# A second group of seven products per feed-forward, with the sums of weight blocks made by adding transfers

## The chip, the cores and the metric

The kernel runs on one core of one Trainium2 chip. The metric is the device time of one execution in microseconds (us), as the median of several runs. The core has five engines that work side by side, each with its own queue of instructions: TensorE (in the profile PE; PEld is its weight load), VectorE (DVE), ScalarE (ACT), GpSimd (POOL) and SyncE (SP), which here only issues transfers. Transfers between the main memory (DRAM) and the on-chip memory run on 16 transfer engines (DMA).

## The reference

A trunk of two layers on 256 tokens of width 1024, all in float32. Each layer is a sandwich of feed-forward, mixer, feed-forward; the first layer's mixer is a convolution module, the second's a latent attention. The change touches the feed-forwards, of which there are four:

```python
def swiglu_ffn(h, w1, w3, w2):
    return (jax.nn.silu(h @ w1) * (h @ w3)) @ w2

for i in range(DEPTH):                       # DEPTH = 2
    h = h + 0.5 * swiglu_ffn(rmsnorm(h, ffn_norm1[i]), ffn1_w1[i], ffn1_w3[i], ffn1_w2[i])
    m = rmsnorm(h, mix_norm[i])
    h = h + (conv_module(m, ...) if i == 0 else mla(m, ...))
    h = h + 0.5 * swiglu_ffn(rmsnorm(h, ffn_norm2[i]), ffn2_w1[i], ffn2_w3[i], ffn2_w2[i])
return rmsnorm(h, final_norm)
```

`w1` and `w3` are 1024 x 2816, `w2` is 2816 x 1024.

## The kernel before

**Blocks.** Weights come as blocks of 128 x 2048 float32 (one megabyte), in a fixed list `blocks`, in the order of use. A block is fetched into one of four raw buffers (tag `raw`, `RAW_BUFS = 4`) and then split into a high part `hi` (a rounding copy on ScalarE) and a low part `lo` (raw minus high, on VectorE), each in two pieces of 1024 columns (`PIECES = 2`). Five pairs of `hi` and `lo` exist (`W_BUFS = 5`). Activations are split in the same way (`Xh`, `Xl`; `Gh`, `Gl`). Every product of two float32 tiles is three matmuls (`mm3`): high times low, high times high, low times high.

**The first product** (`h @ w1` and `h @ w3` together) runs over six chunks `c` of output columns: 0 to 4 with 512 columns of each of the two matrices, 5 with 256. A plain chunk of 512 is four blocks (two halves of the rows of the weights for each matrix). Its 2 x 2 x 2 block products of 12 matmuls are 96 matmuls into four accumulator banks: two matrices by two blocks of 128 tokens.

**A group of seven.** In the chunks listed in `SEVEN_UP`, and in the first four blocks of every second product (`SEVEN_DOWN`), the eight block products of this 2 x 2 by 2 x 2 block matrix product are replaced by seven, in the manner of Winograd and Strassen: some factors are sums of weight blocks, some are sums of row blocks ("forms"), and the results are combined between banks. That makes 84 matmuls. `seven(four)` puts seven entries in the list, `load_seven` makes the j-th factor of the weights, `seven_products` runs the products, `sums_of_rows`, `whole_rows` and `forms_of` make the forms of the rows. Before, there is one such chunk in each first product, chunk 3, and one group in each second product: eight groups. `load_seven` fetches the four blocks once each (L185) and makes four in-place differences of whole blocks on VectorE (L201). The forms of chunk 3 are made when chunk 1 begins; their whole rows take a raw buffer for a while.

**The start of feed-forwards two to four.** The two blocks of 128 tokens become ready one after the other. The rows of the second block are turned by a round trip through DRAM (`turn_blocks`, L489 writes, L494 reads); `X.begin()` first calls `raw_to`, which fills free raw buffers with coming blocks (L181), and then issues these turns. `first_chunk` runs chunk 0 in an order of its own; when its third part is done being laid out, it calls `load_ahead()`, which brings in the blocks up to three ahead of those in use. Fetches in `load` (L239) and `fetched` are ordered behind the last turned read:

```python
dma = nc.sync.dma_start(raw, src)
if turns:
    order(dma, turns[-1].ins)
```

**What sets the order.** The program is laid out by a planner that fills each engine's queue from its own estimate of times, with priority to what stands earlier in the code; `urgent` raises the priority, `order(a, b)` puts a behind b in a queue without a wait at run time. `behind` keeps splits behind the latest urgent instructions. `gates` are the splits of a chunk's outputs after their turn (`turn`, L862); `seven_products` orders them among the weight splits.

## Time and profile before

| | us |
|---|---|
| median of 3 runs | 892.14 (891.55 to 892.82) |
| the profiled execution, whole | 891.44 |
| its span in the trace | 889.5 |
| feed-forward two, first product begins | 272.1 |
| feed-forward three, first product begins | 446.2 |
| feed-forward four, first product begins | 708.7 |

The page shows one profiled execution. Busy time of an engine excludes the instructions that only issue transfers or wait. A group of instructions is given with its line, engine, operation, the names of what it writes and reads, its count, its busy time, the mean duration in ns, and the idle time of its engine before it with what ended that. Rows of stretches give: the stretch, its length, busy time and count for PE, PEld, DVE, ACT and POOL, the granted clock of TensorE, the busy share of the transfer engines, and GB/s. Rows of one line of the code give durations in ns (min/median/max) and the first and last start; "DMA to landing" gives min/median/max from issue to landing. Rows in order of time give start, length, engine, line, operation, count.

### The profile page before, as it was taken

The numbers are of one execution on the slowest core, as the hardware profiler recorded it, in microseconds if no ns is written. First come the engines' busy times: TensorE is split into PE (matmuls) and PEld (weight loads), VectorE is DVE, ScalarE is ACT, GpSimd is POOL, SyncE is SP. The second block draws the span as 40 slices with busy tenths as digits, with TensorE's granted clock in tenths as the row PEclk, the third lists the DMA queues.
The fourth block names the chain that finished last, engine by engine and source line by source line (L and its number), as shares of the span: only waits on it lengthen the run. The fifth ranks groups of instructions, "written<-read, shape, count | busy, mean of one in ns | idle before, by whom it ended". The sixth has DMA issues, their size and how long they took to land.

```text
span 889.5 us, 12294 instructions
## 1 busy us (share of the span) xinstructions
PE 882.0 (99%) x4209; PEld 741.9 (83%) x4209; DVE 770.4 (87%) x1114; ACT 580.2 (65%) x1005; POOL 104.8 (12%) x227
## 2 busy tenths in 40 slices
PE   9999999999999999999999999999999999999997
PEld 7888887898988888888888888888899888888886
DVE  6899999789999998999498989995778689989973
ACT  7667868789887655657275465673676666474752
POOL 1000000079952000000010000001400010000000
PEclk9999999999999999999999999999999999999999
DMA  9884929834216855939759378495643549287541
GB/s 338 297 308 161 398 80 374 300 132 153 96 60 225 307 213 194 365 93 393 251 179 344 97 249 318 142 386 183 221 147 142 190 155 368 80 300 276 192 190 48
DMA packets 71054, 198.94 MB, mean 224 GB/s; under 512 B 12368, under 2 KB 41936, under 8 KB 51664
## 3 DMA queue, kind: packets, MB, share of 16 engines
q1 hardware_dynamic: 70560, 197.47, 61.9%
q8 instruction: 33, 0.54, 0.2%
q10 hardware_dynamic: 432, 0.69, 0.2%
q14 instruction: 29, 0.24, 0.1%
HBM read 181.87 MB, written 16.25 MB: 223 GB/s over the span
## 4 chain that ended last, share of the span: by engine, by line
PE 98%; DVE 1%; issue 0%; ACT 0%; ACTq 0%; DVEq 0%
PE u L333 17%; PE u L337 17%; PE u L336 17%; PE o L333 9%; PE o L337 9%; PE o L336 9%; PE u L1019 3%; PE gate L1019 3%; PE o L1255 3%; PE u L418 2%; PE sc L1616 1%; PE tp L453 1%; PE pairs L1062 1%; DVE lo L201 1%; PE a L337 1%; PE a L336 1%
## 5 line engine op out<-in xcount | busy, mean ns | idle before, releaser
L248 DVE TENSOR_TENSOR lo<-raw,hi 128x1024 fp32r<-128x1024 f32 (+1 forms) x228 | 266.8, 1210 | 29.2 <-ACT hi L247 28.5
L247 ACT CAST hi<-raw 128x1024 fp32r<-128x1024 f32 (+1 forms) x230 | 228.5, 1044 | 72.1 <-DMA raw<-in_f2w 24.3
L337 PE MATMUL u<-hi,Xl 128*128 128x512 f32 x592 | 230.4, 389 | 0.0
L336 PE MATMUL u<-hi,Xh 128*128 128x512 f32 x592 | 230.3, 389 | 0.0
L333 PE MATMUL u<-lo,Xh 128*128 128x512 f32 x592 | 230.2, 389 | 0.0
L215 ACT CAST hi<-raw 128x1024 fp32r<-128x1024 f32 x112 | 111.7, 1049 | 56.7 <-DVE raw L201 46.4
L201 DVE TENSOR_TENSOR lo<-raw,hi 128x1024 fp32r<-128x1024 f32 x112 | 132.0, 1215 | 6.6 <-ACT hi L215 6.5
L337 PEld LDWEIGHTS u<-hi,Xl 128*128 128x128 f32 x592 | 111.1, 188 | 23.6 <-DVE Xl L472 0.5
L336 PEld LDWEIGHTS u<-hi,Xh 128*128 128x128 f32 x592 | 111.1, 188 | 23.1
L333 PEld LDWEIGHTS u<-lo,Xh 128*128 128x128 f32 x592 | 111.1, 188 | 22.9
L333 PE MATMUL o<-lo,Gh 128*128 128x512 f32 (+1 forms) x276 | 106.7, 386 | 0.0
L336 PE MATMUL o<-hi,Gh 128*128 128x512 f32 (+1 forms) x276 | 106.5, 386 | 0.0
L337 PE MATMUL o<-hi,Gl 128*128 128x512 f32 (+1 forms) x276 | 106.5, 386 | 0.0
L444 POOL TENSOR_TENSOR ms<-ss 128x1 f32<-128x1 f32 x16 | 8.1, 509 | 592.8 <-ACT junk L436 592.8
L201 DVE TENSOR_TENSOR raw<-raw,raw 128x2048 f32<-128x2048 f32 x32 | 73.1, 2285 | 0.8 <-DMA raw<-in_f1w 0.2
L333 PEld LDWEIGHTS o<-lo,Gh 128*128 128x128 f32 x276 | 51.8, 188 | 10.6 <-DVE lo L201 0.2
L337 PEld LDWEIGHTS o<-hi,Gl 128*128 128x128 f32 x276 | 51.8, 188 | 10.5
L336 PEld LDWEIGHTS o<-hi,Gh 128*128 128x128 f32 x276 | 51.8, 188 | 10.4
L1108 DVE SCALAR_TENSOR_TENSOR acc<-V,dw,acc 128x128 f32<-128x128 f32 (+1 forms) x174 | 53.9, 390 | 0.0
L970 ACT ACTIVATE s<-u,R 128x512 f32<-128x512 f32 (+1 forms) x48 | 30.9, 647 | 29.5 <-PE u L337 28.7
L1129 ACT ACTIVATE prod<-V,dw 128x128 f32<-128x128 f32 (+1 forms) x128 | 45.6, 415 | 1.9 <-POOL Y L1130 1.0
L806 DVE SCALAR_TENSOR_TENSOR h<-o,rh,h 128x512 f32<-128x512 f32 (+1 forms) x18 | 12.9, 719 | 29.0 <-PE o L337 29.0
(269 smaller groups left out, 1306.6 us busy)
## 6 DMA issues: line engine op xcount, KB each, us to landing
raw<-in_f2w SPq DMA_DIRECT2D x66, 1024.0 KB, 5.6
raw<-in_f1w SPq DMA_DIRECT2D x62, 1024.0 KB, 6.9
raw<-in_cw SPq DMA_DIRECT2D x12, 1024.0 KB, 5.2
gd<-gt SPq DMA_DIRECT2D x160, 64.0 KB, 2.9
gb<-gd SPq DMA_DIRECT2D x24, 256.0 KB, 2.8
rows<-gd SPq DMA_DIRECT2D x16, 256.0 KB, 3.3
raw<-in_wo SPq DMA_DIRECT2D x4, 1024.0 KB, 4.7
hd<-rows SPq DMA_DIRECT2D x56, 64.0 KB, 2.3
```

The source lines that it names most:

```text
L201: ins = nc.vector.tensor_sub(out, left, right)
L215: casts[n, i] = nc.scalar.copy(hi[:, c], raw[:, c]), sub(lo[:, c], raw[:, c], hi[:, c].bitcast(F32))
L247: casts[len(loaded), i] = (nc.scalar.copy(hi[:, c], raw[:, c]), low.tensor_sub(lo[:, c], raw[:, c], hi[:, c].bitcast(F32)))
L248: low.tensor_sub(lo[:, c], raw[:, c], hi[:, c].bitcast(F32)))
L333: mm = nc.tensor.matmul(o, ah, bl, start=start, stop=False, skip_group_check=seeded)
L336: nc.tensor.matmul(o, ah, bh, start=False, stop=False, skip_group_check=seeded)
L337: return nc.tensor.matmul(o, al, bh, start=False, stop=stop, skip_group_check=seeded)
L970: nc.scalar.activation(s[:, :w], u[0, tb][:, :w], AF.Silu, scale=X.r[tb])
L1019: mm = nc.tensor.matmul(u[:, t], w[:, c], X.x[:, k, t], start=(k == 0), stop=(k == KT - 1))
L1108: dve_last.append(nc.vector.scalar_tensor_tensor(out if j == j1 - 1 else y, v, w, y, op0=ALU.mult, op1=ALU.add))
L1129: prods_last.append(nc.scalar.activation(p, v, AF.Copy, scale=w))
L1255: p = nc.tensor.matmul(o[tb, d], (Zl if kind == "x" else Zh)[:, f, tbs(tb)], (lo if kind == "l" else hi)[:, c], start=(f, kind) == (0, "l" ...
```

## The change

`SEVEN_UP` gets chunk 1 beside chunk 3 for feed-forwards two to four: eleven groups instead of eight. The differences of weight blocks become sums, and the sums are made by transfers issued from GpSimd that add into a raw buffer. The signs of the forms and of the combinations between banks are changed to match. Of the four blocks f0 to f3, the group now fetches d = f2, y = f1, c = f0 and x = f0; it adds f3 into y and f1 into x. The seven factors are x, c, d, x, y, c, x: before the fourth, f3 is added into x; before the sixth, c is fetched anew with f3; before the seventh, f2 is added into x. That is five plain and four adding transfers per group, where four plain ones were.

The order of the products changes too: the first is now one with a form of the rows (and x), and product 2 is cut in two halves of six matmuls with product 3 between them. The forms are made at chunk 0 where chunk 1 is a group. `raw_to` now stops at a block that is a tuple (a group's entry). The buffers of the turned blocks with tag `g` become three, the orderings of the gates are fitted, and in the attention the scores of heads one and two are ordered behind those of the head before.

```diff
-SEVEN_UP = {0: (3,), 1: (3,), 2: (3,), 3: (3,)}
+SEVEN_UP = {0: (3,), 1: (1, 3), 2: (1, 3), 3: (1, 3)}
...
     def raw_to(last):
         while len(loaded) + len(raws) < last:
             src = blocks[len(loaded) + len(raws)]
-            assert not isinstance(src, tuple)
+            if isinstance(src, tuple):
+                break
...
-    def fetched(src):
-        raw = rawp.tile([P, HB], F32, tag="raw", name=uid("raw"))
+    def fetched(src, raw=None):
+        if raw is None:
+            raw = rawp.tile([P, HB], F32, tag="raw", name=uid("raw"))
         dma = nc.sync.dma_start(raw, src)
         if turns:
             order(dma, turns[-1].ins)
...
         if j == 0:
-            b[11], b[12] = fetched(four[0]), fetched(four[1])
-        elif j == 1:
-            b[22] = fetched(four[3])
-        elif j == 2:
-            b[21] = fetched(four[2])
...
-        if j == 1:
-            sub(b[11], b[12], b[11])
-            sub(b[12], b[22], b[12])
-        elif j == 2:
-            thirds[n] = sub(b[11], b[22], b[11])
+            b["d"], b["y"], b["c"], b["x"] = (fetched(four[i]) for i in (2, 1, 0, 0))
+            nc.gpsimd.dma_start(b["y"], four[3], accum_op=ALU.add)
+            nc.gpsimd.dma_start(b["x"], four[1], accum_op=ALU.add)
+        elif j == 3:
+            nc.gpsimd.dma_start(b["x"], four[3], accum_op=ALU.add)
+        elif j == 5:
+            fetched(four[3], b["c"])
         elif j == 6:
-            sub(b[11], b[21], b[11])
-        raw = b[(11, 11, 11, 21, 12, 22, 11)[j]]
+            nc.gpsimd.dma_start(b["x"], four[2], accum_op=ALU.add)
+        raw = b["xcdxycx"[j]]
...
-        sums = [(0, x22, x21, x22, ALU.add), (2, x21, x11, x21, ALU.subtract), (1, x11, x22, x11, ALU.subtract),
-                (3, x12, x12, x11, ALU.subtract)]
+        sums = [(0, x22, x21, x22, ALU.subtract), (2, x21, x11, x21, ALU.subtract),
+                (1, x11, x22, x11, ALU.subtract), (3, x12, x12, x11, ALU.add)]
...
-        product(rows(0, 0), c11, True)
-        first = urgent(nc.scalar.copy)(c21, c11)
+        product(0, forms[0], c22, True)
+        kept = tmp.tile([P, 512], F32, tag="s", name=uid("p5"))
+        first = urgent(nc.scalar.copy)(kept, c22)
...
+        product(1, rows(0, 0), c11, True)
+        urgent(nc.scalar.copy)(c21, c11)
+        product(2, rows(1, 0), c11, False, range(2))
+        product(3, forms[1], c21, False)
+        product(2, rows(1, 0), c11, False, range(2, 4))
+        add = urgent(nc.vector.tensor_sub)(c12, kept, c21)
...
+        product(4, forms[2], c21, False)
+        add = urgent(nc.vector.tensor_sub)(c22, kept, c21)
+        product(5, forms[3], c12, False)
...
+        product(6, rows(1, 1), c21, False)
...
-            if seven_up and c == min(seven_up) - 2:
+            if seven_up and c == max(min(seven_up) - 2, 0):
...
-            last = None
+            last = score_last[-1] if 0 < hd < 3 else None
```

More of the change, by code (lines that the diff above doesn't have):

```diff
@@ L387, in seven_products @@
         n0 = n_used[0]
-        before = []
+        before, parts = [], {}
         c11, c21, c12, c22 = banks[0, 0], banks[1, 0], banks[0, 1], banks[1, 1]
-        product(rows(0, 0), c11, True)
-        first = urgent(nc.scalar.copy)(c21, c11)
+        product(0, forms[0], c22, True)
+        kept = tmp.tile([P, 512], F32, tag="s", name=uid("p5"))
+        first = urgent(nc.scalar.copy)(kept, c22)
         for cast in late.values():
             order(cast, first.ins)
-        product(forms[0], c22, True)
-        kept = tmp.tile([P, 512], F32, tag="s", name=uid("p5"))
-        urgent(nc.scalar.copy)(kept, c22)
-        product(forms[1], c21, False)
-        add = urgent(nc.vector.tensor_add)(c12, c21, kept)
-        order(casts[n0 + 5, 0][1], add.ins)
-        for high, low in gates[-2 * NT:-NT] if not late else ():
-            order(low, thirds[n0 + 2].ins)
+        product(1, rows(0, 0), c11, True)
[4 more added lines that the diff above has]
+        add = urgent(nc.vector.tensor_sub)(c12, kept, c21)
+        order(casts[n0 + 6, 0][1], add.ins)
+        for high, low in gates[max(len(gates) - 2 * NT, gates_from[0]):-NT] if not late else ():
+            order(low, casts[n0 + 2, PIECES - 1][1].ins)
         late_gates = []
@@ L411, in seven_products @@
             order(low, casts[n0 + 7, PIECES - 1][1].ins)
-        product(forms[3], c12, False)
-        product(rows(1, 1), c21, False)
+        order(casts[n0 + 7, 0][1], add.ins)
+        product(6, rows(1, 1), c21, False)
     def some(o, kinds, ah, al, bh, bl, start, stop):
```

28 lines of the change are left out of this document (13 added, 15 removed).

## The prediction

> **What bounds the kernel now.** I read the page from the top: the shares, the transfer queues, the chain that ended last, the groups of instructions, the transfer issues.
>
> ```profile
> span 889.5 us, 12294 instructions
> ...
> PE 882.0 (99%) x4209; PEld 741.9 (83%) x4209; DVE 770.4 (87%) x1114; ACT 580.2 (65%) x1005; POOL 104.8 (12%) x227
> ...
> DMA packets 71054, 198.94 MB, mean 224 GB/s; under 512 B 12368, under 2 KB 41936, under 8 KB 51664
> ...
> q1 hardware_dynamic: 70560, 197.47, 61.9%
> ...
> PE 98%; DVE 1%; issue 0%; ACT 0%; ACTq 0%; DVEq 0%
> ...
> L248 DVE TENSOR_TENSOR lo<-raw,hi 128x1024 fp32r<-128x1024 f32 (+1 forms) x228 | 266.8, 1210 | 29.2 <-ACT hi L247 28.5
> L247 ACT CAST hi<-raw 128x1024 fp32r<-128x1024 f32 (+1 forms) x230 | 228.5, 1044 | 72.1 <-DMA raw<-in_f2w 24.3
> ...
> L444 POOL TENSOR_TENSOR ms<-ss 128x1 f32<-128x1 f32 x16 | 8.1, 509 | 592.8 <-ACT junk L436 592.8
> L201 DVE TENSOR_TENSOR raw<-raw,raw 128x2048 f32<-128x2048 f32 x32 | 73.1, 2285 | 0.8 <-DMA raw<-in_f1w 0.2
> ...
> raw<-in_f1w SPq DMA_DIRECT2D x62, 1024.0 KB, 6.9
> ```
>
> The chain is TensorE (PE) for 98% of the span. VectorE (DVE) is busy 87%, and yet nothing waits for it: less VectorE work by itself saves nothing. Only fewer matmuls, or a stall of TensorE, can move the time. What one matmul is worth is its share of a whole first product, not its modelled duration, since matmuls overlap. These are the stretches of busy time of the first products of feed-forwards two, three and four:
>
> ```profile
> 272.10:389.10 117.00, 117.00 (x518) 96.85 (x517) 108.58 (x118) 68.58 (x91) 3.21 (x4) 1.00 0.70 250
> 446.20:563.20 117.00, 117.00 (x518) 96.87 (x517) 107.92 (x118) 69.28 (x92) 3.21 (x4) 1.00 0.65 231
> 708.70:825.70 117.00, 116.98 (x518) 96.55 (x516) 107.39 (x121) 70.85 (x97) 3.35 (x8) 1.00 0.64 227
> ```
>
> The code issues 516 matmuls there (four chunks of 96, one of 84, one of 48; the row counts two more that overlap its edges), without a hole and at a granted clock of 1.00: 117.0/516 = 0.2267 us each. A product of a group of seven (12 matmuls) takes 2.72 us, a plain chunk of 96 takes 21.8 us. So chunk 1, which becomes a group of seven, starts today at 293.9, 468.0 and 730.5.
>
> **The change, part by part.** *Matmuls.* Three chunks go from 96 to 84: 36 x 0.2267 = 8.2 us saved, all on the path. Nothing else in the change can save more than a fraction of a microsecond, since TensorE has no idle time to give back.
>
> *VectorE and ScalarE.* The 32 subtractions on raw blocks go: 32 x 2.285 = 73.1 us of VectorE, off the path, worth 0. Three chunks have seven blocks to split into high and low halves instead of four: 9 blocks, two pieces each, 18 x 1.21 = 21.8 us of VectorE and 18 x 1.04 = 18.8 us of ScalarE, covered by the 51 us that VectorE is relieved of on balance and by ScalarE's idle 35%. Worth 0.
>
> *Where the first transfers of chunk 1 can start.* This is the step that I think decides. Today chunk 1 is plain, and its first raw blocks are fetched ahead by the function that fills the raw buffers before the second token block is turned. In the changed code that function stops at a block of a group. The group's fetches are issued later, and by the ordering in the fetch helper they stand on SP's queue behind the read of the last turned block. That read goes out here (the SP queue in order of time):
>
> ```profile
> 278.83 0.34 SPq L494 DMA_DIRECT2D rows<-hd  x1
> 279.21 13.03 SPq L239 DMA_DIRECT2D raw<-in_f2w  x5
> ```
> ```profile
> 451.69 0.34 SPq L494 DMA_DIRECT2D rows<-hd  x1
> 452.07 14.44 SPq L239 DMA_DIRECT2D raw<-in_f1w  x4
> ```
> ```profile
> 717.96 0.34 SPq L494 DMA_DIRECT2D rows<-hd  x1
> 718.41 0.37 SPq L717 DMA_DIRECT2D gf<-in_gfin  x1
> ```
>
> So t0, the issue of the group's first fetch, is 279.2, 452.1 and 718.4: 14.7, 15.9 and 12.1 us ahead of chunk 1. In that time four fetches (d, y, c, x, in this order, with x last), one adding transfer into x, and the split of x must be done, because the first product uses x. Three fetches issued together at 279.2 landed like this:
>
> ```profile
> L239 SPq DMA_DIRECT2D raw<-in_f2w x3: 364/432/433, 279.2 to 280.2; - x3
> ...
> DMA to landing us min/median/max: 4.9/7.0/8.9
> ```
>
> The first landed at 279.2+4.9 = 284.1, the third at 280.2+8.9 = 289.1: 2.5 us apart. The fourth, x, then lands at t0+12.4.
>
> *The price of an adding transfer.* No transfer of this kind is in the trace; call it A from issue to landing. The lower bound is the best plain megabyte, the upper bound the worst fetch of a group:
>
> ```profile
> L181 SPq DMA_DIRECT2D raw<-in_f2w x5: 327/328/328, 247.4 to 704.8; - x5
> ...
> DMA to landing us min/median/max: 4.7/4.9/7.2
> ```
> ```profile
> L185 SPq DMA_DIRECT2D raw<-in_f2w x16: 327/333/432, 303.5 to 809.0; - x16
> ...
> DMA to landing us min/median/max: 5.3/7.6/9.5
> ```
>
> I take 6.9, the median of the 62 megabyte fetches of this weight tensor (last row of the first fence): same size, same source and destination, with other traffic beside them, as the add into x has the one into y beside it. Bounds 4.7 and 9.5. The Trainium skill (DMA: Bandwidth & Descriptors, "Anatomy of one DMA — SWDGE (gpsimd) path") gives 2.0 us plus the bytes over 436 GB/s for a transfer issued from GpSimd, an estimate of 4.4 us for a megabyte; by it the sum below would be 902. The plain megabytes of this trace never beat 4.7.
>
> *The first product.* The first half of x is split after 1.04 (high) + 1.21 (low) = 2.3 us. Product 0 starts at t0+12.4+6.9+2.3 = t0+21.6: 300.8, 473.7, 740.0, late by 6.9, 5.7 and 9.5 us, together 22.1.
>
> *The later sums in x.* The next add may go out only when the split of x is finished, 1.2 us after its first half; then 6.9 and 2.3 again: 10.4 us from product 0 to product 3. TensorE has 2.5 products between them (0, 1 and half of 2), 6.8 us: a stall of 3.6. From product 3 to product 6 it has 3.5 products, 9.5 us: a stall of 0.9. Together 4.5, times three, 13.5.
>
> *The other eight groups* (chunk 3 and the second product, everywhere) get the same chain, with more time ahead. In chunk 3 of feed-forward three the fetches go out here:
>
> ```profile
> L185 SPq DMA_DIRECT2D raw<-in_f1w x4: 327/340/352, 479.0 to 488.0; - x4
> ...
> DMA to landing us min/median/max: 6.1/7.9/8.1
> ```
>
> The last of the four lands at 488.0+8.1 = 496.1 at worst; +6.9+2.3 = 505.3, against 511.6 for product 0 (446.2 + 3 x 21.8). Product 3 is ready at 515.7 (needed 518.4), product 6 at 526.1 (needed 527.9): hidden, with 1.8 us to spare at the end. I price them at 0; three adds share that margin, so it is gone when A passes 7.5, and at 9.5 each of these groups would stall about 6 us.
>
> *Forms of the rows.* They are now needed by product 0 of chunk 1, and their sum takes a raw buffer, free when d is split:
>
> ```profile
> L352 DVE TENSOR_TENSOR xs<-Xh,Xl 128x2048 f32<-128x2048 f32 x4 | 9.1, 2286 | 0.0
> L345 DVE TENSOR_TENSOR xs<-xs 128x512 f32<-128x512 f32 x16 | 10.9, 683 | 0.0
> ```
>
> d at t0+4.9, split +3.5, sum +2.3, first form +0.7 and its own split about +1.3: t0+12.7, covered by x's chain (t0+21.6). If that cover went, it would still be in time in two of the three.
>
> *Order of the products, copies between banks.* A half product (1.36 us) stands behind each copy or subtraction:
>
> ```profile
> L259 DVE TENSOR_TENSOR u<-u,p x2: 693/696/700, 520.8 to 525.3; 128x512 f32<-128x512 f32 x2
> ...
> L259 ACT COPY u<-u x1: 570/570/570, 514.5 to 514.5; 128x512 f32<-128x512 f32 x1
> ```
>
> 0.57 and 0.70 fit in 1.36: 0. *Queues.* The adds wait on POOL's queue; behind them stand only the norms' small operations (L444), whose next turn comes after the second product's plain blocks. The repeated fetch of c waits on SP for the split of c; behind it stand chunk outputs, not read before the second product. Both 0. The order of two heads' scores and the third buffer for turned blocks move no work: 0.
>
> *Sum.* 22.1 + 13.5 - 8.2 = +27.4 us. The profiled execution took 891.4 us (span 889.5), 0.7 under the median 892.1; so 918.8 against its own time, **919.5** against the median. With A = 4.7: late by 4.7, 3.5, 7.3, and 1.4 at each product 3, +11.5, 904. With A = 9.5: 29.9 + 3 x (6.2+3.5) - 8.2 = +50.8, 943.
>
> **The rivals.** *Faster: the loads go out earlier than I think.* The raw buffers of the group are free long before t0 (today they hold prefetched blocks), and only the order on SP holds the fetches back. Were they issued as the buffers come free, x would land about 10 us sooner, every stall of the first groups would be covered, and the gain of 8.2 would remain: 884. It breaks even when x lands 27.4/3 = 9.1 us earlier in each. Against it: the three pairs of rows above show weight fetches or others right behind that read, as the ordering demands. The groups of chunk 3 show that with more time ahead everything is hidden.
>
> *Slower still: the transfer engines become the bound.* An adding transfer reads its destination as well as its source. If that costs a second megabyte of engine time, a group needs 5 + 4 x 2 = 13 megabytes of it where a chunk needed 4. Full rate, from the stretch of today's chunk 1:
>
> ```profile
> 468.00:489.70 21.70, 21.70 (x97) 17.99 (x96) 18.25 (x22) 11.99 (x15) 0.00 (x0) 1.00 0.90 340
> ```
>
> 340/0.90 = 378 GB/s, 2.78 us per block. Chunks 1 to 3 need 13+4+13 = 30 blocks, 83 us, and 3.1 MB of turned outputs, 8 us: 91 us. There are 71 us from t0 of feed-forward three to the last add of chunk 3 in time. Short by 20, three times, less 8.2: 892 + 52 = 944 or more. The Trainium skill (Collectives: The Full Stack, "The bandwidth ceiling: the fold count and why AG ≠ RS ≠ AR") says that an adding transfer runs at half the rate for just this reason, two source reads on one ring; no run here shows it yet. For it: q1 already fills 61.9% of 16 engines, and 11 groups at 9 transfers in place of 8 at 4 and 3 chunks at 4 add 55 megabyte transfers. Against it: the wait of one add is mostly latency, and the adds of x lie apart.
>
> *No change.* The stalls just eat the gain: 892. It needs a sum of stalls of 8 us, under the 19.7 that even A = 4.7 gives.
>
> **How the numbers follow.** Start-up stall of chunk 1 and its chain: 0.55, 919.5, own range 904 to 943. Engines the bound: 0.28, 944 and up. Faster: 0.12. No change: 0.05. Less than 0.2% cannot be told from no change here. So faster 0.12, same 0.05, slower 0.83. For 8 in 10 the range takes in the likeliest case, most of the second and the edge of no change: 893 to 950.
>
> **What would show it.** TensorE should stand still at the start of chunk 1 of feed-forwards two to four (6 to 10 us), released by a split that waited for an adding transfer into a raw block, and again at its product 3; nothing at chunk 3. SP's row for the group's first fetch should come within 1 us of the last turned read. I am wrong if those fetches are earlier, if adds land in under 4 us, or if TensorE also stops at chunk 3 and in the second products: then the engines' rate, not the start, is the bound, and the share of transfer time in these stretches should read 0.95 or more.

## The result and the profile after

The changed kernel takes **1117.89 us** (median of 4 runs, 1115.7 to 1122.45); the kernel before took 892.4 beside it (891.55 to 892.82). The ratio is 1.2535, with a 95% interval of 1.2489 to 1.2581. The forecast was 919.5, and at most 950: the sign was right, the size was not. The loss is 225 us where 27 were expected.

These are the rows of the page after that answer to those shown of before (span, busy time by engine, transfer queues, the chain that ended last, transfer issues with KB and median us to landing).

```profile
span 1118.1 us, 12382 instructions
...
PE 923.8 (83%) x4173; PEld 760.6 (68%) x4173; DVE 726.6 (65%) x1106; ACT 598.9 (54%) x1029; POOL 145.5 (13%) x271
...
DMA packets 78976, 256.63 MB, mean 230 GB/s; under 512 B 13248, under 2 KB 42816, under 8 KB 52544
...
q1 hardware_dynamic: 72144, 209.01, 52.1%
q0 software_dynamic: 6336, 46.14, 21.3%
...
PE 20%; DMA 14%; DVE 4%; ACT 2%; issue 2%; SPq 1%; ACTq 0%; POOLq 0%
...
raw<-in_f2w POOLq DMA_DIRECT2D x24, 1024.0 KB, 9.0
raw<-in_f1w POOLq DMA_DIRECT2D x20, 1024.0 KB, 9.4
...
gd<-gt SPq DMA_DIRECT2D x160, 64.0 KB, 6.0
gb<-gd SPq DMA_DIRECT2D x24, 256.0 KB, 7.4
```

The 36 matmuls are gone (4209 to 4173), and VectorE is relieved of 44 us. But TensorE was 98% of the chain and is now 20%. The 44 adding transfers (issued by POOL) take 9.0 and 9.4 us from issue to landing, where 6.9 was assumed. The small transfers that carry turned outputs (`gd`, `gb`) were 2.9 and 2.8 us in the profile before and now take 6.0 and 7.4.

What TensorE waited for is in the view of its waits (tile and line, what it waited for: us in total, times, longest):

```profile
PE u L331 <- ACT Gh L364: 82.8, 3, 30.2
PE u L331 <- DVE lo L212: 31.9, 8, 8.3
PE u L331 <- DVE u L257: 23.0, 7, 5.1
PE o L331 <- DVE lo L212: 21.4, 5, 4.9
PE o L331 <- ACT o L257: 18.0, 4, 6.3
PE o L331 <- DVE o L257: 5.6, 2, 4.8
PE u L331 <- ACT u L257: 4.7, 7, 0.7
```

The first row is the start of the three new groups: almost 28 us each, put down to the split of a form of the rows (`Gh`), not to a weight. The others are splits of weight blocks (L212) and copies and subtractions between banks (L257), and they lie in the eight old groups; inside the three new ones there is one copy each, of 0.7 us.

I took the whole loss apart with the starts of successive matmuls: a gap above 0.6 us counts as a stall, a start-to-start time of 0.25 to 0.6 us as slow pitch (a full matmul takes 0.2267).

| us | before | after |
|---|---|---|
| stalls ahead of chunk 1 (feed-forwards 2, 3, 4) | 0 | 27.0 + 25.9 + 30.4 = 83.3 |
| stalls inside chunk 1 | 0 | 2.5 |
| eight old groups: stalls ahead of them | 0 | 41.1 |
| eight old groups: stalls inside them | 0.6 | 66.1 |
| slow pitch | 3.2 | 46.5 |
| matmuls saved | | -8.2 |

The difference of stalls and slow pitch, less 8.2, is 228; the spans differ by 228.6. Nothing is lost outside the feed-forwards. Of the stalls, 107 us lie at the eight old groups, which the forecast priced at nothing.

Stretches of feed-forward two, after: chunk 0 with the stall behind it, chunk 1 (now a group), chunk 2 with the stall ahead of chunk 3, chunk 3, and a part of the first stall (columns as in the section on the profile before).

```profile
308.90:357.70 48.80, 21.98 (x98) 17.86 (x96) 25.10 (x34) 15.91 (x27) 6.75 (x8) 0.77 0.76 216
357.70:380.10 22.40, 21.74 (x84) 17.45 (x85) 17.76 (x22) 17.51 (x22) 0.00 (x0) 0.89 0.82 247
380.10:406.10 26.00, 21.96 (x97) 17.84 (x96) 9.61 (x13) 4.81 (x7) 1.73 (x2) 1.00 0.93 265
406.10:441.60 35.50, 24.43 (x85) 18.20 (x86) 29.00 (x32) 23.37 (x28) 1.73 (x2) 0.86 0.87 270
330.00:358.00 28.00, 1.18 (x5) 0.69 (x4) 14.54 (x14) 8.65 (x10) 2.60 (x3) 0.60 0.71 171
```

Chunk 1 itself then runs through in 22.4 us, against 19.0 for a group before. Of the excess 2.5 is slow pitch: the granted clock reads 0.89 here, after 0.60 in the stall. The transfer engines are busy 0.71 to 0.93, and 0.93 is where chunk 3's own fetches meet its first two additions, while chunk 2 runs.

The first stall in order of time. SP, GpSimd, ScalarE and VectorE (start, length, engine, line, operation, count, idle time before with its releaser):

```profile
315.35 0.34 SPq L495 DMA_DIRECT2D rows<-hd  x1
315.73 2.08 SPq L188 DMA_DIRECT2D raw<-in_f2w  x4
```
```profile
324.68 0.94 POOL L200 DMA_DIRECT2D raw<-in_f2w  x1 [6.82 <-issue]
330.16 0.86 POOL L201 DMA_DIRECT2D raw<-in_f2w  x1 [4.54 <-issue]
344.17 0.86 POOL L203 DMA_DIRECT2D raw<-in_f2w  x1 [13.14 <-DVE lo L212]
356.79 0.88 POOL L207 DMA_DIRECT2D raw<-in_f2w  x1 [11.77 <-DVE lo L212]
```
```profile
340.32 5.78 ACT L211 CAST hi<-raw 128x1024 fp32r<-128x1024 f32 x6 [16.81 <-DMA raw<-in_f2w]
352.94 1.99 ACT L211 CAST hi<-raw 128x1024 fp32r<-128x1024 f32 x2 [6.84 <-DMA raw<-in_f2w]
357.01 1.34 ACT L364 CAST Gh<-xs 128x512 fp32r<-128x512 f32 x2 [2.08 <-DVE xs L343]
```
```profile
341.40 6.90 DVE L212 TENSOR_TENSOR lo<-raw,hi 128x1024 fp32r<-128x1024 f32 x6 [9.00 <-ACT hi L211]
348.33 2.29 DVE L350 TENSOR_TENSOR xs<-Xh,Xl 128x2048 f32<-128x2048 f32 x1
354.02 2.36 DVE L212 TENSOR_TENSOR lo<-raw,hi 128x1024 fp32r<-128x1024 f32 x2 [3.39 <-ACT hi L211]
356.29 1.41 DVE L343 TENSOR_TENSOR xs<-xs 128x512 f32<-128x512 f32 x2
```

The four fetches follow the last turned read by 0.38 us, as forecast. Block x lands at 329.4 (t0+13.7; forecast +12.4). The first addition into x goes out at 330.16 and lands at 340.30: 10.1 us. Then ScalarE and VectorE split x, c and d in one piece of work (to 348.3), VectorE makes the whole rows (to 350.62), and there both engines stop. Next on their queues is the split of the fourth factor, which is x after its second addition (344.17 to 352.84). Only behind it stand the sums of the forms (L343, 356.29), and product 0 wants a form. So product 0 starts at 357.7: it waits for two additions and not for one. By x alone it could have started when the first half of x was split, at about 342.6.

### The profile page after: what moved, and what is told of

Its sections match the earlier page's. It is cut to its first block, busy times and chain, and to the rows that moved or that the text cites. A ratio compares the mean times of both kernels' runs of the same rounds, so it can differ in the third digit from the quotient of the medians.

```text
span 1118.1 us, 12382 instructions
## 1 busy us (share of the span) xinstructions
PE 923.8 (83%) x4173; PEld 760.6 (68%) x4173; DVE 726.6 (65%) x1106; ACT 598.9 (54%) x1029; POOL 145.5 (13%) x271
## 3 DMA queue, kind: packets, MB, share of 16 engines
q0 software_dynamic: 6336, 46.14, 21.3%
## 5 line engine op out<-in xcount | busy, mean ns | idle before, releaser
L212 DVE TENSOR_TENSOR lo<-raw,hi 128x1024 fp32r<-128x1024 f32 x154 | 180.1, 1219 | 150.4 <-ACT hi L211 150.3
L211 ACT CAST hi<-raw 128x1024 fp32r<-128x1024 f32 x154 | 150.3, 1044 | 218.0 <-DMA raw<-in_f2w 131.3
L246 DVE TENSOR_TENSOR lo<-raw,hi 128x1024 fp32r<-128x1024 f32 (+1 forms) x204 | 238.4, 1208 | 31.0 <-ACT hi L245 30.4
L245 ACT CAST hi<-raw 128x1024 fp32r<-128x1024 f32 (+1 forms) x206 | 202.9, 1041 | 53.3 <-DMA raw<-in_f1w 16.7
L331 PE MATMUL u<-lo,Xh 128*128 128x512 f32 x532 | 212.5, 399 | 20.7 <-DVE u L257 16.0
L334 PE MATMUL u<-hi,Xh 128*128 128x512 f32 x532 | 210.3, 395 | 0.0
L335 PE MATMUL u<-hi,Xl 128*128 128x512 f32 x532 | 209.2, 394 | 0.0
L331 PE MATMUL u<-lo,Gh 128*128 128x512 f32 x112 | 52.2, 466 | 121.8 <-ACT Gh L364 82.8
L331 PEld LDWEIGHTS u<-lo,Gh 128*128 128x128 f32 x112 | 24.5, 219 | 133.4 <-ACT Gh L364 84.0
L257 DVE TENSOR_TENSOR s<-s,u 128x512 f32<-128x512 f32 x28 | 19.1, 682 | 77.0 <-PE u L335 77.0
L334 PEld LDWEIGHTS o<-hi,Gh 128*128 128x128 f32 x276 | 53.2, 193 | 10.7
L334 PE MATMUL u<-hi,Gh 128*128 128x512 f32 x112 | 49.7, 444 | 0.0
```

The costliest lines, as they stand in the source:

```text
L211: casts[n, i] = (nc.scalar.copy(hi[:, c], raw[:, c]), nc.vector.tensor_sub(lo[:, c], raw[:, c], hi[:, c].bitcast(F32)))
L212: nc.vector.tensor_sub(lo[:, c], raw[:, c], hi[:, c].bitcast(F32)))
L245: casts[len(loaded), i] = (nc.scalar.copy(hi[:, c], raw[:, c]), low.tensor_sub(lo[:, c], raw[:, c], hi[:, c].bitcast(F32)))
L246: low.tensor_sub(lo[:, c], raw[:, c], hi[:, c].bitcast(F32)))
L257: r = f(*args, **kw)
L331: mm = nc.tensor.matmul(o, ah, bl, start=start, stop=False, skip_group_check=seeded)
```

## Experiments

Each run stands beside the kernel before on the same chip (892.0 to 892.1 throughout). The times are single ones, except where an interval is given. "Stalls" and "slow pitch" are counted as above, in the profiled execution of each; where there are several, it took 1119.9 us for the changed kernel and 904.9 for y_by_transfer. The kernels with plain transfers in place of additions, chain_cut and chain_open leave out sums and so compute something else; only their times count.

| kernel | us | stalls | slow pitch |
|---|---|---|---|
| before | 892.0 | 0.6 | 3.2 |
| changed | 1117.9 | 193.0 | 46.5 |
| plain_from_pool | 1020.0 | 114.9 | 24.4 |
| plain_from_sp | 1032.6 | 120.7 | 31.1 |
| old_groups_only | 1020.3 | 99.3 | 32.0 |
| forms_in_banks | 1119.9 | 175.7 | 63.2 |
| x_first | 1062.8 | 140.1 | 41.5 |
| chain_cut | 1133.6 | 209.0 | 42.5 |
| chain_open | 1076.1 | 150.6 | 44.5 |
| copies_ahead | 1174.3 | 237.8 | 55.4 |
| x_first_copies_ahead | 1048.3 | 122.5 | 44.7 |
| x_first_copies_plain | 949.6 | 48.1 | 20.6 |
| vector_sums | 946.4 | 53.5 | 12.7 |
| vector_sums_banks | 923.5 | 28.6 | 14.0 |
| two_groups_y | 929.3 | 32.5 | 15.9 |
| y_by_transfer | 899.0 | 8.1 | 8.3 |

### Is it the addition itself?

**plain_from_pool**: the four additions become plain transfers, with everything else as it is.

```diff
-            nc.gpsimd.dma_start(b["x"], four[1], accum_op=ALU.add)
+            nc.gpsimd.dma_start(b["x"], four[1])
...
```

> The four adding transfers of each group become plain ones from the same queue, which overwrite the raw block: the sums are left out, all waits and the order stay. Theory A (an adding transfer costs a second read: its packets take 629 ns where plain ones take 309): from issue to landing inside a group falls from 8.4 us by eight packets x 320 ns = 2.6 us to about 5.9, each group's chain through x shortens by that three times, and the time falls from 1118 to about 1000. Theory B (it is GpSimd's way of issuing that is slow, not the addition): the landings and the time stay, 1110 or more.

Measured: 1020.04, near theory A. From its page:

```profile
q0 software_dynamic: 6336, 46.14, 12.5%
...
raw<-in_f2w POOLq DMA_DIRECT2D x24, 1024.0 KB, 6.6
raw<-in_f1w POOLq DMA_DIRECT2D x20, 1024.0 KB, 6.5
```

The same 6336 packets and the same bytes took 21.3% of 1118.1 us of engine time when they added and take 12.5% of 1018.3 when they don't: 238 against 127, or 1.87 times. Landing falls from 9.2 to 6.6 us in the median of all 44, and the kernel gains 100 us on the changed kernel's profiled 1119.9. So what an addition costs beyond a plain transfer is a real cause, for somewhat under half of the loss. The other half stays although a transfer now takes, in the median, less than the 6.9 of the forecast.

**plain_from_sp**: the same plain transfers, issued from SP.

```diff
-            nc.gpsimd.dma_start(b["x"], four[1], accum_op=ALU.add)
+            nc.sync.dma_start(b["x"], four[1])
...
```

> As the one before, with the four plain transfers issued by SyncE instead of GpSimd (sums left out again). Theory A: about 1 us less per transfer (GpSimd's 0.87 us of issuing), so a small further gain, 970 to 1000. Theory B: nearly all of the loss goes only here, 900 to 930.

Measured: 1032.55. It is no better than from GpSimd, 12.5 us worse; both theories missed it. That the transfers come from GpSimd's queue is not the cause.

**old_groups_only**: the changed kernel with chunk 1 plain again.

```diff
-SEVEN_UP = {0: (3,), 1: (1, 3), 2: (1, 3), 3: (1, 3)}
+SEVEN_UP = {0: (3,), 1: (3,), 2: (3,), 3: (3,)}
```

> The changed kernel without the second group: chunk 1 is plain again, the eight old groups keep the adding transfers. Theory A with the chain through x (each group stalls by itself, whatever else is transferred): the stalls at the start of chunk 1 go (27.0 + 25.9 + 30.4 = 83 us, and about 7 us of slow matmuls behind them), the saving of 8.2 goes too, and the rest stays: about 1036. Theory C (the transfer engines are full, all groups stall for lack of rate): with 27 fewer transfers the groups at chunk 3 of feed-forwards two to four nearly stop stalling too, 980 or less.

Measured: 1020.33, nearer to theory A. The eight old groups lose 128 us by themselves, 16 each. Chunk 3 of feed-forward two shows how; GpSimd's additions there (the first is into y, the other three into x), and the stretches of chunk 2 and of chunk 3:

```profile
352.89 0.94 POOL L200 DMA_DIRECT2D raw<-in_f2w  x1 [34.97 <-PE u L335]
358.44 0.86 POOL L201 DMA_DIRECT2D raw<-in_f2w  x1 [4.61 <-DMA raw<-in_f2w]
373.02 0.86 POOL L203 DMA_DIRECT2D raw<-in_f2w  x1 [13.72 <-DVE lo L212]
386.65 0.88 POOL L207 DMA_DIRECT2D raw<-in_f2w  x1 [12.77 <-DVE lo L212]
```
```profile
352.30:374.10 21.80, 21.80 (x98) 18.05 (x97) 5.93 (x7) 6.93 (x9) 2.66 (x3) 1.00 0.80 218
374.10:405.20 31.10, 21.20 (x85) 16.77 (x84) 24.82 (x29) 18.47 (x23) 0.88 (x1) 0.89 0.92 273
```

Block x landed at 357.7, 16.4 us ahead of product 0; the forecast had 15.5. The three additions into x landed at 369.09, 382.10 and 395.85: 10.7, 9.1 and 9.2 us, together 28.9 where 20.7 were forecast. Between them lie 3.9 and 4.6 us from landing to the next issue, where 3.5 were forecast. Product 0 is in time; TensorE stops for 7.6 us ahead of product 2, where it waits for a copy that stands behind the split of the second sum, and for 2.6 ahead of product 6. This is the chain of the forecast with a higher price, in the place where it was priced at 0: 9.7 us longer than forecast, where 1.8 were to spare, and 10.2 us of stalls.

### Is it the start of chunk 1?

**forms_in_banks**: the whole rows for chunk 1's forms are summed into two accumulator banks and two temporary tiles (`rows_in_banks`) and not into a raw buffer, so that they don't wait for one.

```diff
+                whole = rows_in_banks(X.xh, X.xl) if c == 0 else whole_rows(X.xh, X.xl, after)
+                forms = forms_of(sums_of_rows(*whole), Gh[:, 14:], Gl[:, 14:])
```

> The changed kernel, only that the whole rows for the forms of chunk 1 stand in two accumulator banks and two small buffers instead of a raw buffer, so that the forms need not wait for d's buffer nor stand behind the splits of the group. Theory D (at the start of chunk 1 half of the stall is the forms' place in the queues, behind the split of the fourth factor, which waits for the second addition): the stall there falls from 27, 26 and 30 us to what x alone asks, about 12, 11 and 15, and the time to about 1070. Theory E (the two additions into x set that stall by themselves): no change, 1110 to 1125.

Measured: 1119.87, no gain, in the range of theory E, though not for its reason. In feed-forward two the stall ahead of chunk 1 falls from 27.0 to 12.4 us, but those inside chunk 1 rise from 0.8 to 12.1 and the slow pitch from 2.5 to about 6. Product 6 starts 67.1 us after chunk 0 began, where it was 68.5: TensorE now waits inside the group, ahead of product 2 for a copy that stands behind the split of the second sum, and ahead of product 6 for a subtraction that ran at 377.21, behind other splits on VectorE, though the third addition had landed at 370.34. A wait that ends last at a place isn't yet a cause of the time.

**x_first**: as forms_in_banks, and x is fetched first and its addition issued ahead of that into y.

```diff
-            b["d"], b["y"], b["c"], b["x"] = (fetched(four[i]) for i in (2, 1, 0, 0))
-            nc.gpsimd.dma_start(b["y"], four[3], accum_op=ALU.add)
+            b["x"], b["c"], b["d"], b["y"] = (fetched(four[i]) for i in (0, 0, 2, 1))
             nc.gpsimd.dma_start(b["x"], four[1], accum_op=ALU.add)
+            nc.gpsimd.dma_start(b["y"], four[3], accum_op=ALU.add)
```

> As forms_in_banks, with the four fetches of a group in the order x, c, d, y in place of d, y, c, x, and the addition into x issued ahead of the one into y. By the chain through x, x lands three transfers (7.5 us) sooner where the four fetches go out together, as at the start of chunk 1, and its first addition no longer shares the engines with the one into y: the stall there falls from 12, 12 and 15 us to 2 to 6, while y is late instead only if it lands after product 4 needs it. Over three groups some 25 to 30 us: 1085 to 1100. If the start of chunk 1 hung on something else than x: 1115 or more.

Measured: 1062.81, 57 us better than forms_in_banks and more than expected. The stall ahead of chunk 1 is now 5.8 to 8.0 us, and ahead of chunk 3 and of the second product there is almost none. But additions take 11.8 us in the median. Why is not shown: those that overlap with another addition take no longer than the rest (11.4 and 12.2). The waits inside the groups carry another name:

```profile
PE u L331 <- ACT u L257: 56.1, 7, 12.3
PE o L331 <- ACT o L257: 39.1, 4, 13.3
```

### Is it the chain through one buffer, or the rate?

**chain_cut**: the second and third additions go into d, so that x's splits needn't wait for them (the factors are then other sums than the group's).

```diff
-            nc.gpsimd.dma_start(b["x"], four[3], accum_op=ALU.add)
+            nc.gpsimd.dma_start(b["d"], four[3], accum_op=ALU.add)
...
-            nc.gpsimd.dma_start(b["x"], four[2], accum_op=ALU.add)
+            nc.gpsimd.dma_start(b["d"], four[2], accum_op=ALU.add)
```

> The changed kernel with the same eleven groups and the same transfers, but the additions of f3 and f2 that belong into x go into d's buffer, which is dead by then: factors 4 and 7 take x without these sums (they are left out), and their splits need not wait for an addition. Theory A with the chain (split, add, split, add in one buffer paces a group): the stalls inside the groups, some 10 us in each of the eight old ones and hidden behind the late start of the three new ones, go, and most of the slow matmuls behind them; the stalls ahead of the first product, which hang on the first addition alone, stay: 960 to 1010. Theory C (the engines lack rate; the bytes are the same): 1080 or more.

Measured: 1133.58, worse. The stalls inside the old groups are about halved (3.8 to 6.8 us in chunk 3, 3.0 to 6.0 in the second product). But d's buffer is now held by additions, and chunk 1's whole rows need it: that start stall grows to 38.4, 37.6 and 40.9. The run mixes two effects and decides nothing.

**chain_open**: on top of forms_in_banks, the splits read c where they read x for the fourth and seventh factor. The additions go on, but no product waits for the last two into x.

```diff
-        raw = b["xcdxycx"[j]]
+        raw = b["xcdcycc"[j]]
```

> As forms_in_banks, with all eleven groups and all adding transfers into x in their places, but factors 4 and 7 are split from c's buffer instead of x (their values are left out), so that no split waits for the second and third addition and no buffer is held longer. Theory A with the chain through x: the stalls inside the groups (about 12 us in each new group, 9 in chunk 3, 7 in the second product) and most of the slow matmuls behind them go; what hangs on the first addition stays (12 to 15 us ahead of chunk 1, 3 to 9 ahead of the old groups): 960 to 1000. Theory C (the bytes of the adding transfers are what limits): 1080 or more.

Measured: 1076.12, 44 us better than forms_in_banks and between the two theories. Inside the groups of feed-forwards two to four the stalls fall (chunk 1 from about 12, chunk 3 from 6 to 11, both to about 4 or less). Ahead of the next group they rise: 9.6 to 12.5 us ahead of chunk 3. Additions take 10.3 and 10.5 us. So the chain paces TensorE inside a group; when it doesn't, the next group's x is late. In feed-forward two x of chunk 3 goes out last, at 377.70, when a split frees its buffer; it lands 11.4 us later, beside y's addition, and its own addition takes 8.8, so that product 0 starts at 401.1. Whether buffers or the rate of the transfers hold it back is not separated. Neither theory stands alone.

**copies_ahead**: two orderings more in the changed kernel, which put the copy after product 1 and the second subtraction ahead of the splits that wait for an addition.

```diff
-        urgent(nc.scalar.copy)(c21, c11)
+        copy = urgent(nc.scalar.copy)(c21, c11)
+        order(casts[n0 + 3, 0][0], copy.ins)
...
         add = urgent(nc.vector.tensor_sub)(c22, kept, c21)
+        order(casts[n0 + 6, 0][1], add.ins)
```

> The changed kernel, with two orderings more: on ScalarE the copy between banks after product 1 stands ahead of the split of the fourth factor, and on VectorE the second subtraction between banks stands ahead of the split of the seventh factor. Nothing else differs. Theory Q (order on the engines): TensorE's waits put down to copies and subtractions between banks are 23.0 + 18.0 + 5.6 + 4.7 = 51 us in the changed kernel, because these small instructions stand behind splits that wait for an adding transfer. With the subtraction ahead, product 6 starts when the seventh factor is split, some 4 us earlier in six groups (22 us); with the copy ahead only half a product (1.4 us) can run before product 3 wants the same split, in three groups (4 us). So about 1090, 1085 to 1105. Theory G (what a group gains its successor gives back, since the next group's fetches are paced by the transfers): 1110 to 1122.

Measured: 1174.33, 54 us worse than the changed kernel's 1119.9; both theories missed it. GpSimd in chunk 1 of feed-forward two:

```profile
348.06 0.86 POOL L203 DMA_DIRECT2D raw<-in_f2w  x1 [13.56 <-DVE lo L212]
372.41 0.88 POOL L207 DMA_DIRECT2D raw<-in_f2w  x1 [23.49 <-DVE lo L212]
```

The third addition goes out 24.4 us after the second, where it was 12.6 (344.17 and 356.79 above). In chunk 1 the second sum of x is ready before product 0 starts; its split now stands behind a copy that waits for product 1, and the third addition waits for that split. An early step of the chain was tied to TensorE. The stalls ahead of chunk 3 of feed-forward two rise from 4.2 to 10.7 us. In the whole kernel the waits for copies and subtractions did fall, from 51.3 to 33.3, while those for splits rose from 53.3 to 113.2.

**x_first_copies_ahead**: the same two orderings in x_first, where the fourth factor is not ready early.

```diff
+        copy = urgent(nc.scalar.copy)(c21, c11)
+        order(casts[n0 + 3, 0][0], copy.ins)
...
+        order(casts[n0 + 6, 0][1], add.ins)
```

> The kernel of x_first (x fetched and added first, rows of chunk 1's forms through banks) with the two orderings of copies_ahead. In x_first 95 us of TensorE's waits are put down to the copies between banks on ScalarE. If these waits are only the cover of the wait for the second addition into x (the copy stands behind the split that waits for it), moving the copies saves half a product per group, 11 x 1.4 = 15 us, and the subtractions little: 1040 to 1050. If the order on ScalarE is itself the cost, most of the 95 us go: under 1000.

Measured: 1048.3, 14.5 us better than x_first, as the theory of a cover has it. Waits of TensorE in this kernel:

```profile
PE u L331 <- DVE lo L212: 39.7, 10, 7.9
PE u L331 <- ACT u L257: 34.8, 7, 9.5
PE o L331 <- ACT o L257: 26.7, 4, 9.5
```

The 95.2 us put down to copies have become 61.5, and the splits' share has grown: most of the wait was for the addition behind it.

**x_first_copies_plain**: and with plain transfers in place of the adding ones.

```diff
-            nc.gpsimd.dma_start(b["x"], four[1], accum_op=ALU.add)
+            nc.gpsimd.dma_start(b["x"], four[1])
...
```

> x_first_copies_ahead with plain transfers in place of the adding ones, still from GpSimd and with the same waits (the blocks are not summed: each transfer overwrites its buffer). It shows what is left of the chain when the second read, the order of the fetches and the order of the copies are all taken away. From the plain-transfer run (1020): 61 us of stalls ahead of chunk 1 become about 15 by the order of fetches, and some 15 go with the copies: about 950, 935 to 970. If it stays above 990, the three are not the main causes and the chain through one buffer is dear at any rate of transfer; if it comes under 920, the chain costs next to nothing once additions are as quick as plain transfers.

Measured: 949.57, as expected (950). Transfers into x and y take 6.8 and 7.4 us (median by weight tensor). Ahead of chunk 1 TensorE stands still for 3.9, 2.9 and 5.2 us, and inside each of the eleven groups for 2.2 to 4.8. In size this is what the forecast described, with its price of 6.9 per transfer: it had 4.5 for a group. But it shows in all eleven groups, not in three, and the chain isn't its only cause. In each of the eleven groups, here and in the changed kernel, TensorE stops for 0.8 us or more ahead of product 2, which adds into the bank that the copy after product 1 is reading. The changed kernel in chunk 1 of feed-forward two:

```profile
365.78 0.57 ACT L257 COPY u<-u 128x512 f32<-128x512 f32 x1 [0.27 <-PE u L335]
366.40 0.50 PE L331 MATMUL u<-lo,Xh 128*128 128x512 f32 x1 [0.66 <-ACT u L257]
```

The copy starts at once and nothing stands between the two products, where the order before had a product into another bank. Eleven times 0.8 is 9 us, about what the removed matmuls save; no run takes this wait away. And the transfer engines are nearly full in chunk 3 of feed-forwards two to four of this kernel (third figure from the right: granted clock; then their share and GB/s):

```profile
351.50:373.70 22.20, 20.36 (x86) 15.41 (x84) 18.84 (x23) 14.26 (x17) 0.53 (x1) 1.00 0.97 358
540.00:561.50 21.50, 19.82 (x85) 15.36 (x84) 18.79 (x24) 14.60 (x18) 0.54 (x1) 1.00 0.98 364
824.50:848.90 24.40, 21.47 (x87) 16.59 (x86) 20.37 (x25) 15.47 (x19) 0.53 (x1) 0.93 0.94 344
```

Taken one after the other, from below, the loss of 228 us is then:

| step | us |
|---|---|
| what is left at the plain price: the chain through x, more transfers on nearly full engines, the copy after product 1, slow pitch, less 8.2 saved | 57.6 (892.0 to 949.6) |
| additions in place of plain transfers | 98.7 (to 1048.3) |
| copies and subtractions behind waiting splits | 14.5 (to 1062.8) |
| x fetched last, its addition second | 57.1 (to 1119.9, forms_in_banks) |

The cost of adding came out the same at the other end of this row: 99.8 from the changed kernel to plain_from_pool. The smaller terms depend on the order in which they are taken, as copies_ahead shows.

### Does the second group pay with sums on VectorE?

**vector_sums**: the kernel before, with chunk 1 as a second group, and all sums as before on VectorE.

```diff
-SEVEN_UP = {0: (3,), 1: (3,), 2: (3,), 3: (3,)}
+SEVEN_UP = {0: (3,), 1: (1, 3), 2: (1, 3), 3: (1, 3)}
...
```

> The kernel before with the second group alone: chunk 1 of feed-forwards two to four becomes a group, its sums stay on VectorE, no transfer adds. Three times 12 matmuls less are 8.2 us. VectorE has 153 us of work in the 174 us of feed-forward three; four sums and three more blocks to split add 16.5 us, so it would be full (169 of 171). If VectorE is no limit: 884. If the new group waits for its forms, whose raw buffer comes free only when the group's fourth block is split, or VectorE falls behind: 890 to 910.

Measured: 946.35. Neither 884 nor 890 to 910 held. The stalls around chunk 1 are 13.8, 12.9 and 15.2 us, put down to the split of a form, and chunk 3 stalls some 3 us.

**vector_sums_banks**: and the whole rows in banks, as in forms_in_banks.

```diff
...
+                whole = rows_in_banks(X.xh, X.xl) if c == 0 else whole_rows(X.xh, X.xl, after)
...
```

> As vector_sums, with the rows for the forms of chunk 1 in accumulator banks and small buffers, so that the forms wait for no raw buffer. If the raw buffer was the wait, this comes to 884 to 890; if VectorE is the limit, it is no better than vector_sums.

Measured: 923.49, between the two expectations: the raw buffer was one wait, not the only one. Chunk 1 of feed-forward two, and what TensorE waited for:

```profile
295.70:321.20 25.50, 21.86 (x85) 16.62 (x85) 25.50 (x27) 17.53 (x21) 0.00 (x0) 0.93 0.47 167
```
```profile
PE u L335 <- DVE lo L203: 14.3, 10, 3.5
```

VectorE is busy for 25.50 of 25.50 us while TensorE needs 19.0: in this chunk the work of VectorE, which had cost nothing, is the bound. The transfer engines idle half of the time (0.47). So the thought behind the change, to take sums from VectorE, fits this stage; the price of the transfers in the other stages outweighs it.

**y_by_transfer**: the kernel before with one addition per group, the one into y, which is outside the chain; the sums in x stay on VectorE (with the signs of the changed kernel).

```diff
-            sub(b[12], b[22], b[12])
+            nc.gpsimd.dma_start(b[12], four[3], accum_op=ALU.add)
...
```

> The kernel before, one group per first product, with one of the four sums of a group made by an adding transfer, the one into y, which no later sum waits for and which product 4 needs last; the three in x stay on VectorE. If only the chain of additions through x costs time, an adding transfer of 9 us with 20 us ahead of it is hidden: 892, and VectorE has 18 us less to do. If adding transfers hurt by their load on the engines: 897 or more.

Measured: 899.0 (median of 6, 898.2 to 904.85) against 892.06 (median of 7), ratio 1.007 with an interval of 1.0054 to 1.0087. It lies where load on the engines was expected (897 or more). The profiled execution, with 904.9 the longest of the six, has three stalls of 1.7 to 3.8 us at the groups; the other additions are hidden. It costs 7 us and gains nothing, since VectorE wasn't waited for.

**two_groups_y**: y_by_transfer and vector_sums_banks together.

```diff
+SEVEN_UP = {0: (3,), 1: (1, 3), 2: (1, 3), 3: (1, 3)}
...
+            nc.gpsimd.dma_start(b[12], four[3], accum_op=ALU.add)
...
+                whole = rows_in_banks(X.xh, X.xl) if c == 0 else whole_rows(X.xh, X.xl, after)
```

> As vector_sums_banks (second group, sums on VectorE), with the sum into y made by an adding transfer in all groups. VectorE has 2.3 us less in each of three groups of a feed-forward. If VectorE is what the second group lacks, the stalls in chunks 1 and 3 shrink by about that: 900 to 910; if it is not VectorE: 920 or more. Under 892 it would be faster than the kernel before.

Measured: 929.33, beside 923.49 without the additions, where it was expected if VectorE is not what lacks (920 or more). Chunk 1 of feed-forward two does get shorter (25.5 to 23.2 us), but chunk 3 gets longer (23.1 to 26.9). No version found is faster than the kernel before.

## Why the prediction was wrong

*What held.* The matmuls saved (36, 8.2 us). The issue of the group's fetches right behind the last turned read (0.38 us). Block x's landing (t0+12.5 to 13.7 for +12.4). The chain of addition, split, addition through x. That nothing outside the feed-forwards moves. The rival of earlier fetches (884) fell with the second of these, and that of no change (892) with the stalls.

*The price of an addition.* 6.9 us was taken from plain transfers; it is 9.0 to 9.4 in the median, and 11.5 and 10.2 for the first ones of a group, into y and into x. The upper bound of 9.5 was right for the median alone, and the reason stood in the rival, not in the term: an addition keeps the transfer engines busy nearly twice as long. Of the 9.2, 2.6 are this: each of the 16 engines has eight packets per megabyte, 320 ns longer each, and 2.6 is also what the landing fell by in plain_from_pool. The Trainium skill (Collectives: The Full Stack, "The bandwidth ceiling: the fold count and why AG ≠ RS ≠ AR") gives half the rate for two source reads on one ring, measured there on a collective (ReduceScatter against AllGather). The runs agree in the main, for the transfers of one core: 1.87 times the engine time for the same bytes, and about 100 us of the kernel. That it is the read and not the adding, no run here separates. (Two small figures were off, and nothing hangs on them: the least plain megabyte before took 4.6 us, not 4.7, and the 71 us of the second rival are 71.7 by its own times.)

*The eight old groups, priced at 0.* This is the largest error. They cost 128 us by themselves. The text had said that at A = 9.5 each would stall about 6 us, but the sum at that bound (943) counted only the three new groups. Those 48 us would have made it 991, outside the range that was given. A margin of 1.8 us over three serial transfers is no cover when the transfer's price is unknown by 2.6. But the price is not all: with plain transfers of about 7 us (x_first_copies_plain) these groups still stalled 2.2 to 4.1 us each.

*Forms of the rows, "covered".* The step was timed as if each engine took up what was ready. VectorE and ScalarE took up what stood next in their queues (VectorE was idle from 350.62 to 354.02 with the whole rows made), and the forms stood behind the split of the fourth factor, a whole addition later. The stall ahead of chunk 1 was 27 us, not 7; x alone would have made it about 12. Moving the forms moved the stall without shortening the kernel. What mattered was the order in which x is fetched and added to (57 us between forms_in_banks and x_first, in all eleven groups).

*Copies between banks, priced at 0.* The forecast had half a product behind each. Behind the copy after product 1 there is none, since product 2 adds into the bank that it reads: at least 0.8 us in each group, 9 us in all, about as much as the matmuls saved. Altogether 51 us of waits are put down to copies and subtractions in the changed kernel, most of them because they stand behind splits that wait for transfers. These are mostly a cover: putting the copies first gave 14.5 us in x_first.

*Slower matmuls, not priced.* Slow pitch costs 43 us more than before. It is a consequence of the stalls, and should have been added to every one of them.

*The rival "transfer engines become the bound"* (944 or more) holds the result in its open range. Its first half, the doubled engine time, is shown. Of its second half, the sign that TensorE also stops at chunk 3 and in the second products came true, but the busy share of the transfer engines reads 0.76 to 0.93 in these stretches of the changed kernel, not 0.95. Yet in x_first_copies_plain, where the order of fetches and copies is another, it reads 0.94 to 0.98 in chunk 3, even with plain transfers. An estimate by the prediction's own figures (2.78 us a block, 8 us for outputs) says why: chunks 1 to 3 need 22 blocks or 69 us of the engines at the plain price, and 30 or 91 us with additions, while their products take 60. In x_first_copies_plain the three chunks took 69.1, 67.4 and 73.8 us. So by this estimate the change asks for more transfers than these chunks can hide, chain or no chain. How much of the loss is the chain and how much the rate stays open, and so does what latency and queueing make of the 6.6 us that an addition takes besides its own longer packets.

## What to carry to other kernels

Work moved from an engine that nobody waits for to a transfer buys nothing, and it takes on the transfer's latency; where several such transfers go through one buffer, each with a split between, count the whole chain in every place where it is used, with an upper price for each link, and compare it with the products that cover it. When an operation waits in an in-order queue, all behind it waits too: time the steps in the order of the queues, not by when their inputs are ready. The wait that the profile names is where the time was spent, and only a run that takes it away tells whether the time goes with it (here most of such waits reappeared under another name). Count also the engine time of all transfers in a stage against its products before counting any single wait.

## What the runs showed of the hardware

An adding transfer costs the transfer engines nearly a second transfer: of 8192-byte packets, the median was 309 ns plain and 629 ns adding in the changed kernel. Small transfers in the same kernel get slower too: 64 KB from 2.9 to 6.0 us, 256 KB from 2.8 to 7.4. Only a part of it comes from adding: with plain transfers in the same places they took 4.8 and 4.7.

TensorE pays for a stall after its end. In the changed kernel the ten gaps of 0.5 to 2 us were followed by 1.1 us of slow pitch in all, the seven of 2 to 3.4 us by 4.7, and the nineteen longer ones by 40.3, or 2.1 each. The granted clock was 0.89 and 0.86 over the two groups of the first product of feed-forward two, and 1.00 in the plain chunk between. The Trainium skill (TensorE: Matmul & The Clock Gate, "HAM oscillation — how this bites in real kernels") warns of idle gaps above some 3.4 us for this reason. The rows agree for the nineteen, each followed by 1.4 us or more; but of the seven shorter ones two, of 2.3 and 2.7 us, were also followed by 1.7.

Who issues a plain megabyte hardly matters here: 1020 us from GpSimd, 1033 from SP.
